# Thirty-two bytes over on the tiles of split weights and of the activations' pool

## The chip, the cores and the metric

The kernel runs on one core of a Trainium2 chip. The metric is the device time of one execution in microseconds (us), the median of several runs. Engines are named as in the profile: PE is TensorE, DVE is VectorE, ACT is ScalarE, POOL is GpSimd, and SP issues transfers.

## The reference

A decoder trunk of two layers on 256 tokens of width 1024, float32. Cut to what matters:

```
for each of 2 layers:
  h += 1/2 * (silu(n1 @ Wg1) * (n1 @ Wu1)) @ Wd1            # n1 = RMSNorm(h), hidden width 2816
  P  = RMSNorm(h) @ W_in                                    # one projection to all four mixers and the gates
  y  = retention(P), mamba2(P), latent_attention(P), differential_attention(P)   # each 256 x 512
  h += (sum_i sigmoid(gate_i) * (y_i @ W_branch_i)) @ W_out
  h += cross_attention(RMSNorm(h), RMSNorm(mem)) @ W_o      # 4 heads of 256
  h += 1/2 * (silu(n2 @ Wg2) * (n2 @ Wu2)) @ Wd2
return RMSNorm(h)
```

## The kernel before

Every large product is done in three passes of `float32r` matmuls. An operand is split into a part `hi` that fits `float32r` and a rest `lo`, and the product is hi·hi + lo·hi + hi·lo. For activations the function `split` (L346) makes the two parts, for weights `fetch` (L316) does: SP fetches a tile of 128 x 2048 numbers into `wr`, ACT copies it as `float32r` into `wh` (L334), and DVE subtracts to make `wl` (L335), in two halves. Each of the three pools `wr`, `wh` and `wl` has three buffers, so that one tile is used while the next is split and a third arrives.

`linear` (L351) holds activations as the stationary operand (`lhsT`, 128 x 128) and streams the weights (`rhs`, 512 columns); for each tile of weights and each of the two blocks of tokens it issues four matmuls of `wh` with `hi`, four of `wh` with `lo` and four of `wl` with `hi`:

```
for part, w in ((0, hi), (1, hi), (0, lo)):
    for k in range(m):
        pe.matmul(p_[b][:, :n], lhsT=xT(part, k0 + k)[:, b * P:(b + 1) * P], rhs=w[:, k * n:(k + 1) * n], ...)
```

`linear_t` (L371) is the other way round: the weights are stationary and 256 tokens are streamed, so the result comes transposed.

The activations come from two places. Normalized and transposed inputs of a stage are `xh0`, `xl0`, `xh1`, `xl1`, one buffer each of 128 x 1024 in the pool `xp`. Everything else of that size (`hid` of the feed-forward stages, the mixers' inputs and results such as `yrh` or `ymh`, the normalized memory `mmh`/`mml`, the cross attention's `xk`, `xq`, `xp`, `xo`) comes from `m4` (L171), a ring of eleven buffers in the pool `mp`. The pool `fp` has temporaries, among them a ring of five buffers of 128 x 512 handed out by `f2` (L180); `sp` has small tiles by name, handed out by `small` (L186).

The pools lie one behind the other in each partition's memory, in the order in which they are made: `cp` (constants and the residual `h`), `wr`, `wh`, `wl`, `xp`, `fp`, `sp`, `mp`. Inside a pool the tiles lie one behind the other, a tile's size rounded up to 32 bytes, and all the pools together fill nearly the whole of it. The order of the work is written out by hand: linears follow one another, and "chains" of smaller steps (transposes, softmax, the mixers' small matmuls) are advanced between them. The tables that both layers share (`tables`, L524) are one such chain near the start; the product `lp` of the differential attention's lambda belongs to it (L567 to L570).

Of the kernel before, what the change touches and what calls it, by code (L numbers as in the profile page):

```python
# [12 lines left out]
F32R = mybir.dt.float32r  # L13
# [3 lines left out]
PSUM = bass.MemoryType.PSUM  # L17
AX = mybir.AxisListType

P = 128  # L20
# [10 lines left out]
BUCKETS = 32  # L31
# tiles of weights that are made ready before the matmuls that are traced
AHEAD = 1

# columns of w_in by use
_sizes = (256, 256, 512, 512, 512, 1024, 8, 256, 128, 32, 512, 512, 512, 4096)
_at = np.concatenate([[0], np.cumsum(_sizes)])
(O_RQ, O_RK, O_RV, O_RG, O_Z, O_XBC, O_DT, O_CQ, O_CKV, O_KR, O_DQ, O_DK, O_DV, O_GL) = (int(v) for v in _at[:-1])
# groups of 512 columns, in the order in which they are streamed
G_QK, G_RV, G_RG, G_X0, G_X1, G_Z, G_DQ, G_DK, G_DV, G_GL = range(10)  # L40
_groups = [O_RQ, O_RV, O_RG, O_XBC, O_XBC + 512, O_Z, O_DQ, O_DK, O_DV] + [O_GL + 512 * i for i in range(8)]
MISC = 256 + 128 + 32 + 8

# per-partition parameters of one layer: (name, columns)
_pcols = [("ffn1", 8), ("mix", 8), ("xa", 8), ("mem", 8), ("ffn2", 8), ("ssm", 4), ("qn", 2), ("kvn", 1), ("dn", 1),
          ("cw", 32), ("cb", 8)]
# parameters that every partition needs, of one layer
_bcols = [("dtb", 8), ("alog", 8), ("dsk", 8), ("lam", 256)]
# [11 lines left out]
BO, NBC = _offsets(_bcols)  # L60
# constants that depend on shapes alone
CO, NCC = _offsets([("ident", 128), ("tri", 384), ("dmask", 256), ("inv", 48), ("sel", 8), ("dec", 4 * 256)])
# [37 lines left out]
def lay(x, mem, positions, **w):  # L100
    """The program's inputs: the arrays given, laid out; and constants."""
    a = {k: np.asarray(v) for k, v in w.items()}
# [45 lines left out]
def program(tc, a, out, upto="all"):  # L148
# [22 lines left out]
    def m4(name, dtype=F32):  # L171
        return mp.tile([P, 1024], dtype, tag="m", name=name)

# [14 lines left out]

    # ---- inputs that stay
    h = [[cp.tile([P, 512], F32, tag=f"h{b}{c}", name=f"h{b}{c}") for c in range(2)] for b in range(NB)]  # L190
# [31 lines left out]

    # ---- the order of work: linears one after another, and chains of smaller steps between them.
    # A chain yields how many half tiles of weights it lets pass, or what has to have happened before it goes on.
    chains = []
# [37 lines left out]

    # ---- weights, fetched in the order of use
    def chunks(srcs, kt, n):
# [43 lines left out]
    todo = list(plan())  # L309
    # a recent instruction of VectorE, for what is to be spread over the linears  # L310
    paced = None
    fetched = []
    # the last of the instructions that split weights, for what is to be queued behind it
    last = None

    def fetch(first=False):  # L316
        """The next tile of weights, as two float32r parts whose sum they are. The first one comes in pieces."""
        nonlocal last
        if not todo:
            return  # L320
        src, n = todo.pop(0)
        r = wr.tile([P, 2048], F32, tag="wr", name="wr")
        hi = wh.tile([P, 2048], F32R, tag="wh", name="wh")
        lo = wl.tile([P, 2048], F32R, tag="wl", name="wl")
        pieces = 4 if first else 2
        if not first:
            nc.sync.dma_start(r[:, :n], src)
        for i in range(pieces):
            s = slice(i * n // pieces, (i + 1) * n // pieces)
            if first:  # L330
                if i == 2:
                    nc.sync.dma_start(h[1][0], a["x"][1, :, :512])
                nc.sync.dma_start(r[:, s], src[:, s])
            last = act.activation(hi[:, s], r[:, s], AF.Copy)  # L334
            dve.tensor_tensor(lo[:, s], r[:, s], hi[:, s].bitcast(F32), ALU.subtract)  # L335
        fetched.append((hi, lo, n))
# [7 lines left out]

    # ---- building blocks
    def split(hi, lo, src):  # L346
        """hi + lo = src, in float32r; src is in SBUF or PSUM."""
        act.activation(hi, src, AF.Copy)
        dve.tensor_tensor(lo, src, hi.bitcast(F32), ALU.subtract)

    def linear(kt, n, xT, evacs):  # L351
        """Rows of tokens times weights [kt * 128, n], one or more; evac(b, psum) takes a block of rows."""
        ps = [[lin.tile([P, 512], F32, tag="lin", name="lin") for _ in range(NB)] for _ in evacs]
# [17 lines left out]
    def linear_t(xT, evac):  # L371
        """Weights [1024, 512] transposed times tokens: evac(i, psum) takes 256 columns as [128, 2, 256]."""
        ps = [lin.tile([P, 512], F32, tag="lin", name="lin") for _ in range(2)]
        for k0 in (0, 4):
            ws = weights(2048)
            for i in range(2):
                begin()
                for j in range(2):
                    for part, w in ((0, 0), (1, 0), (0, 1)):
                        for k in range(4):  # L380
                            o = k * 512 + (i * 2 + j) * P
                            # a start clears the flags of the whole bank: one for both halves
                            pe.matmul(ps[i][:, j * 256:(j + 1) * 256], lhsT=ws[w][:, o:o + P], rhs=xT(part, k0 + k),  # L383
# [6 lines left out]
    def transpose4(src, n=4):  # L390
        """Blocks of 128 columns of src, transposed, in one bank: [128, n, 128]."""
        ps = bank("tr")
# [4 lines left out]
    def split_gain(hi, lo, ps, gain, n=4):  # L397
        """hi + lo = a PSUM tile [128, n, 128] times a gain for each partition and n."""
        t = f2("sgt")[:, :n * P].rearrange("p (k t) -> p k t", k=n)
# [6 lines left out]
    def rstd_of(ss, n, m, name):  # L406
        """(ss / n + eps) ** -0.5 of m columns."""
        t = small("rs" + name, m)
# [9 lines left out]
    class Transposed:  # L418
        """src(b, c): [tokens, 512] for two blocks of columns, transposed and split; with a gain for each column.
        Each half starts as its columns are there."""  # L420

# [41 lines left out]
    def rows_of(r, name):  # L463
        """A value for each token, [P, NB], as rows [P, 256] alike on every partition."""
        ps = bank("rowp")
# [56 lines left out]

    # ---- tables that both layers share
    def tables():  # L524
# [19 lines left out]
        for b in range(NB):  # L544
# [18 lines left out]
            yield 2  # L563
        # lambda of the differential attention: -lambda for each layer
        for l in range(L):
            lp = bcol(l, "lam").rearrange("p (i e d) -> p i e d", i=2, e=2)
            pr = small("lp", 128).rearrange("p (i d) -> p i d", i=2)  # L567
            dve.tensor_tensor(pr, lp[:, :, 0], lp[:, :, 1], ALU.mult)
# [6 lines left out]
            dve.tensor_scalar(nlam[:, l:l + 1], nlam[:, l:l + 1], li, None, ALU.subtract)  # L575
        # relative bias, times 8, with the causal mask: [queries, head, (block 0, keys 0) (block 1, keys 0 and 1)]
        rel = relt[:, :384]
# [9 lines left out]
        for i, t in enumerate(_thresholds()):  # L587
            yield 3
            # not around the change of stage
            while 60 <= now < 72:  # L590
# [8 lines left out]
    def rope(dst, src, tb, n_heads, hf):  # L599
        """dst = src rotated, [P, heads, 2 * hf]; tb: [cos, sin, -sin] of hf columns each."""  # L600
        s = src.rearrange("p h (e d) -> p h e d", e=2)
# [12 lines left out]
    def attend(b, scores, masks, scale, sbt):  # L614
        """Softmax numerators of a block of queries, in sbt [P, n, 256]; the sums' reciprocals. scores: PSUM for each."""
        n, nk = len(scores), (b + 1) * P
# [10 lines left out]
    def probs_t(pT, b, probs):  # L627
        """Transposed probabilities of a block of queries; pT: keys 0 [P, 4, 256] and keys 1 [P, 4, 128]."""
        for kb in range(b + 1):
# [5 lines left out]
    def mixers(l, xT, nxt):  # L635
# [10 lines left out]

        # -- retention
        qk = [f2("qk") for _ in range(NB)]
# [61 lines left out]

        # -- MLA's low ranks, and Mamba's steps
        dtx = small("dtx", 16).rearrange("p (b h) -> p b h", b=2)
# [23 lines left out]
        def mamba():  # L736
            yield ["misc"]
            x = dtx.rearrange("p b h -> p (b h)")
            e, z1, z2, p_ = (small(n, 16) for n in ("sp0", "sp1", "sp2", "sp3"))
            # softplus(x) = max(x, 0) + 2 artanh(e / (2 + e)) with e = exp(-|x|)  # L740
            dve.scalar_tensor_tensor(e, x, -1.0, x, ALU.mult, ALU.min)
# [24 lines left out]
            dve.tensor_copy(gc, pg[:, :16])  # L766
            # the running sums in two parts, for each block of tokens
            gr = sp.tile([P, NB, 16], F32R, tag="gr", name="gr", bufs=1)
# [3 lines left out]
            yield ["x0", "x1"]  # L772
            # xs on tokens
            xdt, xD = two("xdt"), two("xD")
# [65 lines left out]

        # -- Mamba-2: convolution, on channels
        for j in range(2):
# [19 lines left out]

        # -- gates and merge
        mg = []
# [30 lines left out]

        # -- MLA
        qT, kT, v = heads("mqT"), heads("mkT"), two("mv")
# [68 lines left out]

        # -- differential attention
        def on_rows(dst, name):
# [75 lines left out]

    # ---- memory, normalized, transposed and split
    def memory(l, mem, before):
# [187 lines left out]
```

## Time and profile before

| | |
|---|---|
| time, median of 3 runs | 1603.86 us (1603.84 to 1603.92) |
| span of the profiled execution | 1601.6 us, 20813 instructions |
| between that span and the median of the runs | 2.3 us |
| busy: PE, DVE, ACT, POOL | 99%, 67%, 52%, 2% of the span |
[...]
| share of the 16 DMA engines, weights' queue | 50.2% |

The span runs from the first to the last instruction of one profiled execution. Busy time of PE counts overlapping matmuls, so a PE that is busy all the time may still run at different paces.

### The profile page before, as it was taken

The page shows a single profiled execution, that of the slowest core. Times are in us where ns is not written, and L with a number is a line of the kernel's source. Part 1 is how long each engine was busy: PE and PEld are TensorE (multiplying, and loading weights), DVE is VectorE, ACT ScalarE, POOL GpSimd, SP SyncE. Part 2 cuts the span into 40 slices and gives each one's busy share as a digit, 9 for nine tenths or more (in the row PEclk, how much of TensorE's full clock was granted, in tenths as well). Part 3 has the DMA queues.
Part 4 walks back from the last instruction along what each step waited for, and adds up shares of the span by engine and source line. Part 5 has one row for each costly group of instructions (what it writes and reads, how often), then busy time and mean ns, then how long its engine had stood idle before and what let it go on. Part 6 is the DMA issues. An engine that isn't in the chain of part 4 may idle for free.

```text
span 1601.6 us, 20813 instructions
## 1 busy us (share of the span) xinstructions
PE 1587.3 (99%) x8236; PEld 1349.4 (84%) x8236; DVE 1070.4 (67%) x1698; ACT 825.2 (52%) x1221; POOL 27.0 (2%) x39
## 2 busy tenths in 40 slices
PE   8999999999999999999999999999999999999998
PEld 6888889898888988888888888898988899888886
DVE  6787699998777666554465546697656766565543
ACT  6544446656655545444454444475575554454432
POOL 0000000000000000000000000000000000000000
PEclk9999999999999999999999999999999999999999
DMA  7555554454555544555555556444545554455541
GB/s 288 200 178 187 185 175 159 151 169 147 204 184 169 181 155 162 184 184 175 186 192 185 183 174 207 149 158 152 184 150 206 184 183 163 155 177 180 195 171 66
DMA packets 41713, 281.58 MB, mean 176 GB/s; under 512 B 4624, under 2 KB 5008, under 8 KB 9488
## 3 DMA queue, kind: packets, MB, share of 16 engines
q1 hardware_dynamic: 39600, 275.07, 50.2%
q10 hardware_dynamic: 2016, 5.19, 1.0%
q8 instruction: 64, 1.05, 0.3%
q14 instruction: 33, 0.27, 0.0%
HBM read 279.20 MB, written 1.05 MB: 175 GB/s over the span
## 4 chain that ended last, share of the span: by engine, by line
PE 98%; ACT 0%; DMA 0%; issue 0%; DVE 0%; SPq 0%; POOLq 0%; POOL 0%
PE lin L365 78%; PE lin L383 11%; PE tr L394 2%; PE ht L500 1%; PE xs L1094 1%; PE xo L1140 1%; PE up L905 1%; PE my L821 0%; PE ds L990 0%; DMA h<-x 0%; PE ms L941 0%; PE pt L632 0%; ACT wh L334 0%; PE my L823 0%; PE do L1013 0%
## 5 line engine op out<-in xcount | busy, mean ns | idle before, releaser
L335 DVE TENSOR_TENSOR wl<-wr,wh 128x1024 fp32r<-128x1024 f32 (+2 forms) x534 | 624.9, 1195 | 388.1 <-ACT wh L334 385.6
L334 ACT ACTIVATE wh<-wr 128x1024 fp32r<-128x1024 f32 (+2 forms) x534 | 533.4, 1033 | 518.5 <-PE lin L365 398.7
L365 PE MATMUL lin<-wh,xh 128*128 128x512 f32 (+1 forms) x1216 | 334.0, 396 | 0.2 <-ACT wh L334 0.2
L365 PE MATMUL lin<-wh,xl 128*128 128x512 f32 (+1 forms) x1216 | 325.9, 390 | 0.0
L365 PE MATMUL lin<-wl,xh 128*128 128x512 f32 (+1 forms) x1216 | 325.1, 389 | 0.0
L365 PEld LDWEIGHTS lin<-wh,xl 128*128 128x128 f32 x1216 | 228.8, 188 | 48.1
L365 PEld LDWEIGHTS lin<-wl,xh 128*128 128x128 f32 x1216 | 228.8, 188 | 47.7
L365 PEld LDWEIGHTS lin<-wh,xh 128*128 128x128 f32 x1216 | 222.5, 189 | 43.6 <-ACT wh L334 1.2
L365 PE MATMUL lin<-wh,hid 128*128 128x512 f32 x704 | 180.4, 396 | 0.0
L365 PEld LDWEIGHTS lin<-wh,hid 128*128 128x128 f32 x704 | 131.6, 188 | 31.4
L365 PE MATMUL lin<-wl,hid 128*128 128x512 f32 x352 | 97.7, 395 | 0.0
L365 PEld LDWEIGHTS lin<-wl,hid 128*128 128x128 f32 x352 | 66.1, 188 | 16.0
L510 ACT ACTIVATE sg<-lin,rffn 128x256 f32<-128x256 f32 x88 | 40.9, 464 | 65.2 <-PE lin L365 65.1
L596 DVE SCALAR_TENSOR_TENSOR bias<-relt,d,bias 128x384 f32<-128x384 f32 x124 | 69.8, 612 | 0.8
L383 PE MATMUL lin<-xh,wh 128*128 128x256 f32 x384 | 63.2, 287 | 0.0
L383 PE MATMUL lin<-xh,wl 128*128 128x256 f32 x384 | 61.7, 283 | 0.0
L383 PE MATMUL lin<-xl,wh 128*128 128x256 f32 x384 | 61.7, 283 | 0.0
L511 DVE SCALAR_TENSOR_TENSOR toks<-lin,rffn,sg 128x256 f32<-128x256 f32 x88 | 42.3, 481 | 25.7 <-ACT sg L510 25.7
L383 PEld LDWEIGHTS lin<-xh,wh 128*128 128x128 f32 x384 | 53.1, 191 | 0.3
L383 PEld LDWEIGHTS lin<-xh,wl 128*128 128x128 f32 x384 | 53.0, 192 | 0.0
L383 PEld LDWEIGHTS lin<-xl,wh 128*128 128x128 f32 x384 | 52.9, 191 | 0.0
L416 ACT ACTIVATE junk<-h 128x512 bf16<-128x512 f32 x36 | 22.4, 621 | 31.2 <-DVE h L484 17.2
(385 smaller groups left out, 1536.7 us busy)
## 6 DMA issues: line engine op xcount, KB each, us to landing
wr<-gu SPq DMA_DIRECT2D x87, 1024.0 KB, 5.0
wr<-win SPq DMA_DIRECT2D x68, 1024.0 KB, 5.0
wr<-dn SPq DMA_DIRECT2D x40, 1024.0 KB, 4.8
wr<-wbr SPq DMA_DIRECT2D x16, 1024.0 KB, 4.9
wr<-w_out SPq DMA_DIRECT2D x8, 1024.0 KB, 4.9
wr<-xa_wk SPq DMA_DIRECT2D x8, 1024.0 KB, 5.0
wr<-xa_wq SPq DMA_DIRECT2D x8, 1024.0 KB, 4.9
wr<-xa_wv SPq DMA_DIRECT2D x8, 1024.0 KB, 4.9
```

Of the source, the lines that this page charges most:

```text
L334: last = act.activation(hi[:, s], r[:, s], AF.Copy)
L335: dve.tensor_tensor(lo[:, s], r[:, s], hi[:, s].bitcast(F32), ALU.subtract)
L365: pe.matmul(p_[b][:, :n], lhsT=xT(part, k0 + k)[:, b * P:(b + 1) * P], rhs=w[:, k * n:(k + 1) * n], start=first, stop=last)
L383: pe.matmul(ps[i][:, j * 256:(j + 1) * 256], lhsT=ws[w][:, o:o + P], rhs=xT(part, k0 + k), start=k0 + k + part + w + j == 0, stop=k0 + k = ...
L394: pe.transpose(ps[:, k * P:(k + 1) * P], src[:, k * P:(k + 1) * P], ident)
L416: act.activation(j[:, :src.free_size()], src, AF.Square, accum_out=out_)
L500: pe.transpose(ps[:, k, blk(b)], toks[:, b, k * P:(k + 1) * P], ident)
L510: act.activation(sg, ps[:, :256], AF.Silu, scale=xT.r[:, b:b + 1])
L511: paced = dve.scalar_tensor_tensor(toks[:, b], ps[:, 256:], xT.r[:, b:b + 1], sg, ALU.mult, ALU.mult)
L596: dve.scalar_tensor_tensor(bias[:, hd], ge, d8[:, hd, i + 1:i + 2], bias[:, hd], ALU.mult, ALU.add)
L905: pe.matmul(ps[:, :n], lhsT=lowT[p_][:, k0 + k, blk(b)], rhs=wm[w][:, o + k * n:o + (k + 1) * n], start=i == 0, stop=i == len(seq) - 1)
L1094: pe.matmul(ps[:, j], lhsT=q[part][:, 2 * j + k, blk(b)], rhs=kT[c][w][:, 2 * j + k], start=not part + w + k, stop=w + k == 2)
```

## The change

Three kinds of tiles are allocated with 8 more columns of 4 bytes, and used without them: those of `wh`, of `wl`, and the eleven buffers of `m4`. The small tile `lp` (128 columns) is no longer one of `sp`'s but takes a buffer of the ring of `f2`. The rest of the diff drops comments.

```
     def m4(name, dtype=F32):
-        return mp.tile([P, 1024], dtype, tag="m", name=name)
+        return mp.tile([P, 1024 + 8], dtype, tag="m", name=name)[:, :1024]
...
         r = wr.tile([P, 2048], F32, tag="wr", name="wr")
-        hi = wh.tile([P, 2048], F32R, tag="wh", name="wh")
-        lo = wl.tile([P, 2048], F32R, tag="wl", name="wl")
+        hi = wh.tile([P, 2048 + 8], F32R, tag="wh", name="wh")[:, :2048]
+        lo = wl.tile([P, 2048 + 8], F32R, tag="wl", name="wl")[:, :2048]
...
             lp = bcol(l, "lam").rearrange("p (i e d) -> p i e d", i=2, e=2)
-            pr = small("lp", 128).rearrange("p (i d) -> p i d", i=2)
+            pr = f2("lp")[:, :128].rearrange("p (i d) -> p i d", i=2)
```

## Rows read from the trace of the kernel before

**Rows 1.** The page's first lines: span, busy time, share of the span and instructions of each engine; and the granted TensorE clock in 40 slices of the span, in tenths.

```profile
span 1601.6 us, 20813 instructions
PE 1587.3 (99%) x8236; PEld 1349.4 (84%) x8236; DVE 1070.4 (67%) x1698; ACT 825.2 (52%) x1221; POOL 27.0 (2%) x39
...
PEclk9999999999999999999999999999999999999999
```

**Rows 2.** The page's chain that ended last, shares of the span by engine and by line.

```profile
PE 98%; ACT 0%; DMA 0%; issue 0%; DVE 0%; SPq 0%; POOLq 0%; POOL 0%
PE lin L365 78%; PE lin L383 11%; PE tr L394 2%; PE ht L500 1%; PE xs L1094 1%; PE xo L1140 1%; PE up L905 1%; PE my L821 0%; PE ds L990 0%; DMA h<-x 0%; PE ms L941 0%; PE pt L632 0%; ACT wh L334 0%; PE my L823 0%; PE do L1013 0%
```

**Rows 3.** Groups of matmuls by line and shape: engine, operation, out<-in by the program's names, shape, count | busy us, mean ns of one | idle before. Of the 18 groups of 32 on `y` and `xo` tiles the first and the last stand here.

```profile
L365 PE MATMUL lin<-wh,xh 128*128 128x512 f32 x1184 | 326.6, 397 | 0.2 <-ACT wh L334 0.2
L365 PE MATMUL lin<-wh,xl 128*128 128x512 f32 x1184 | 318.4, 391 | 0.0
L365 PE MATMUL lin<-wl,xh 128*128 128x512 f32 x1184 | 317.6, 390 | 0.0
...
L365 PE MATMUL lin<-wh,hid 128*128 128x512 f32 x704 | 180.4, 396 | 0.0
...
L365 PE MATMUL lin<-wl,hid 128*128 128x512 f32 x352 | 97.7, 395 | 0.0
...
L383 PE MATMUL lin<-xh,wh 128*128 128x256 f32 x384 | 63.2, 287 | 0.0
L383 PE MATMUL lin<-xh,wl 128*128 128x256 f32 x384 | 61.7, 283 | 0.0
L383 PE MATMUL lin<-xl,wh 128*128 128x256 f32 x384 | 61.7, 283 | 0.0
...
L383 PE MATMUL lin<-mmh,wh 128*128 128x256 f32 x128 | 20.0, 278 | 0.0
...
L365 PE MATMUL lin<-wh,mmh 128*128 128x512 f32 x64 | 17.9, 400 | 0.0
...
L365 PE MATMUL lin<-wh,ymh 128*128 128x512 f32 x32 | 9.1, 406 | 0.0
...
L365 PE MATMUL lin<-wl,xo1h 128*128 128x512 f32 x32 | 8.7, 394 | 0.0
```

**Rows 4.** Timeline of PE in a gate and up projection, 62.6 to 74.5 us: start in us, us from the first start to the last end of the group, engine, line, out<-in, count. The pace is the distance between two starts.

```profile
62.64 0.60 PE L500 MATMUL ht<-ident,toks 128*128 128x128 f32 x4
63.00 1.17 PE L365 MATMUL lin<-wh,xh 128*128 128x512 f32 x4
64.01 1.09 PE L365 MATMUL lin<-wh,xl 128*128 128x512 f32 x4
64.93 1.07 PE L365 MATMUL lin<-wl,xh 128*128 128x512 f32 x4
65.84 1.07 PE L365 MATMUL lin<-wh,xh 128*128 128x512 f32 x4
...
73.10 1.07 PE L365 MATMUL lin<-wl,xh 128*128 128x512 f32 x4
74.01 0.60 PE L500 MATMUL ht<-ident,toks 128*128 128x128 f32 x4
```

**Rows 5.** The same view of the last down projection, 1538 to 1602 us, first and last of the rows used; 204 matmuls lie between the starts at 1540.88 and 1588.47.

```profile
1540.88 2.03 PE L365 MATMUL lin<-wh,hid 128*128 128x512 f32 x8
...
1588.47 2.03 PE L365 MATMUL lin<-wh,hid 128*128 128x512 f32 x8
```

**Rows 6.** The same view of `linear_t`: on `xh`/`xl` (251 us) and on `mmh`/`mml` (514 us).

```profile
250.93 0.64 PE L383 MATMUL lin<-xh,wl 128*128 128x256 f32 x4
251.41 0.64 PE L383 MATMUL lin<-xh,wh 128*128 128x256 f32 x4
...
514.15 0.62 PE L383 MATMUL lin<-mmh,wl 128*128 128x256 f32 x4
...
516.42 0.28 PE L383 MATMUL lin<-mml,wh 128*128 128x256 f32 x1
```

**Rows 7.** The same view of the cross attention's scores, 550 to 553 us, first row and the row behind the last (24 matmuls between).

```profile
550.00 0.64 PE L1094 MATMUL xs<-xk0h,xq 128*128 128x256 f32 x4
...
552.83 0.41 PE L383 MATMUL lin<-xh,wh 128*128 128x256 f32 x2
```

**Rows 8.** The two groups that split weights, by line and shape, columns as in rows 3, with what ended the idle time before them.

```profile
L335 DVE TENSOR_TENSOR wl<-wr,wh 128x1024 fp32r<-128x1024 f32 x502 | 600.2, 1220 | 368.0 <-ACT wh L334 367.3
L334 ACT ACTIVATE wh<-wr 128x1024 fp32r<-128x1024 f32 x502 | 511.5, 1053 | 484.5 <-PE lin L365 371.0 <-issue 85.3 <-PE lin L383 22.6
```

**Rows 9.** The instructions on the tile `lp`: line, engine, operation, count: duration in ns min/median/max, first and last start in us.

```profile
L568 DVE TENSOR_TENSOR lp<-bcs x2: 285/285/285, 35.5 to 37.0; 128x128 f32<-128x128 f32 x2
L570 DVE TENSOR_REDUCE ls<-lp x2: 280/280/280, 36.3 to 38.5; 128x2 f32<-128x128 f32 x2
```

**Rows 10.** The timeline of PE at 424 columns (240 to 249 us, first row and the row behind the last, 48 matmuls between) and at 384 columns (328.67 us; six up to the next row shown).

```profile
239.82 0.94 PE L365 MATMUL lin<-wh,xh 128*128 128x424 f32 x4
...
249.10 1.04 PE L394 MATMUL tr<-ident,yr 128*128 128x128 f32 x8
...
328.67 0.52 PE L905 MATMUL up<-wh,lowh 128*128 128x384 f32 x2
...
329.73 0.28 PE L905 MATMUL up<-wh,lowh 128*128 128x256 f32 x1
```

## The prediction

> **What bounds the kernel now.** I read the page's first lines, then its chain, then the groups of instructions, then stretches of the timeline of TensorE (PE). The page says that PE is busy for 99% of the span at the full granted clock [rows 1]. The chain that ended last is PE for 98%, of which 78% are the matmuls of line 365 (`linear`) and 11% those of line 383 (`linear_t`) [rows 2]: the time is the number of matmuls times the pace at which one follows another. Busy time doesn't show that pace: the mean of one matmul is 390 to 397 ns because neighbours overlap [rows 3]. The pace is the distance between the starts of two groups in the timeline, divided by the matmuls between them.
>
> Read so, matmuls of one width have more than one pace:
> - 512 columns, stationary operand from the tiles `xh`/`xl`, moving operand from `wh`/`wl`: the first twelve after a break by transposes take 2.84 us (63.00 to 65.84), then 32 take 7.26 us, 226.9 ns each. Over 64.01 to 74.01, with most of the recovery in it, 10.00 us / 44 = 227.3 ns [rows 4].
> - 512 columns, stationary operand from the pool `mp` (`hid`): from 1540.88 to 1588.47, 47.59 us for 204 matmuls, 233.3 ns, right from the first group on [rows 5].
> - 256 columns (`linear_t`): with `xh` as moving operand 0.48 us for four, 120.0 ns; with `mmh`/`mml` (pool `mp`) 2.27 us for 20, 113.5 ns [rows 6]. At L1094, where the operands come from `mp` and `mg`, 2.83 us for 24, 117.9 ns [rows 7].
>
> Clock, shape and data type are alike within each width. What differs is where the operands lie, and that is what the change moves.
>
> **Where the tiles lie.** I add up the tiles in the order of the pools. `wr`, `wh`, `wl`, `xp` and `fp` hold only multiples of 512 bytes, so all their tiles begin at one place of a 512-byte line; call it 0. The small tiles of `sp` add up to 320 bytes more than a multiple of 512, so each tile of `mp` begins at 320. "Moving less stationary" is then 0 for `linear` on `xh`/`xl`, 192 for `linear` on `hid` and its like, 0 for `linear_t` on `xh`/`xl`, and 320 for `linear_t` on `mmh`/`mml`.
>
> After the change the three buffers of `wh` begin at 0, 32 and 64, those of `wl` at 96, 128 and 160, all of `xp` and `fp` at 192 (six times 32). `sp` loses 512 bytes with `lp`, so the eleven buffers of `mp` begin at 0, 32, ... 320. No pair of a weight tile and an `xh`/`xl` tile begins at one place any more (moving less stationary: 320 to 480). With an `mp` tile the difference takes many values, and is 0 for 6 of the 66 pairs.
>
> **The change part by part.**
> 1. *No instruction is added or removed.* Shapes, queues and waits stay; `n` elements of each padded tile are used as before.
> 2. *ScalarE and VectorE write `wh` and `wl` at other places.* Line 334 takes 1053 ns and line 335 takes 1220 ns for 1024 columns; VectorE is busy for 67% of the span, and before these instructions the two engines sat idle for 368 and 485 us, mostly waiting for PE [rows 8]. I cost a change here at nothing: the work that hides it is PE's. Were line 335 a tenth slower, its 600 us would grow by 60 us inside 368 us of slack. No row shows such a loss.
> 3. *`lp` moves from `sp` to the ring of five `f` buffers.* Its four instructions take 285 and 280 ns each on VectorE at 35.5 to 38.5 us [rows 9], and by the code only the norm's four `sgt` tiles have used the ring by then. They queue on VectorE as before: nothing either way.
> 4. *`linear` on `xh`/`xl`*, 3 × 1184 = 3552 matmuls of 512 columns [rows 3], now 227.3 ns. The trace has no such matmul with unequal starts. From below: the pace stays, nothing. From above: the pace of the only 512-column matmuls with unequal starts, 233.3 ns, +6.0 ns × 3552 = +21.3 us. Between them lie the matmuls of 424 and 384 columns. At 424 columns each next `k` moves the moving operand by 1696 bytes, 160 past a multiple of 512, so they see several differences in turn: 9.28 us for 48, 193.3 ns, and they don't settle. At 384 columns (difference 192) six take 1.06 us, 176.7 ns [rows 10]. That is 16.6 ns for 40 columns; carried on by 88 columns it gives 193.3 + 36.6 = 230 ns for 512. After the change the difference holds for four or eight matmuls, then steps by 96 bytes between `wh` and `wl`: partly like the `hid` rows, partly like the 424 rows. I take the middle, 231.65 ns: +4.35 × 3552 = +15.5 us.
> 5. *`linear` on tiles of `mp`*: 704 + 352 on `hid`, 3 × 64 on `mmh`/`mml`, 18 groups of 32 on `y` and `xo` tiles, 1824 together [rows 3], now 233.3 ns. From above: they stay, 0. From below: those find the pace of `xh`, −6.0 × 1824 = −10.9 us. With a different pair of places for nearly every tile they come nearest to the 424 columns, 230 ns: −3.3 × 1824 = −6.0 us.
> 6. *`linear_t`*: 1152 matmuls on `xh`/`xl` [rows 3] leave equal starts. From 120.0 to 113.5 would be −7.5 us, staying is 0; the nearest row is L1094's 117.9 ns, unequal starts that don't settle lower: −2.1 × 1152 = −2.4 us. 384 on `mmh`/`mml` [rows 3] lose their settled 113.5 for the same 117.9: +4.4 × 384 = +1.7 us; bounds 0 and, at 120.0, +2.5 us.
>
> Sum: 15.5 − 6.0 − 2.4 + 1.7 = **+8.8 us**. The span shown is 1601.6 us, and 2.3 us lie around it up to the median of 1603.86; no part of the change touches these. 1603.9 + 8.8 = 1612.7 us. The bounds together: −10.9 − 7.5 = −18.4 (1585.5) and 21.3 + 2.5 = +23.8 (1627.7).
>
> The rows show 120.0 and 113.5 ns for the same 256-column shape with operands in different tiles. [...]
>
> **The rivals.**
> *A: equal starts are the harm (faster).* [...] For it: at 256 columns equal starts are the slowest, 120.0 against 117.9 and 113.5 [rows 6, 7]. Against it: at 512 columns equal starts are the fastest, 226.9 against 233.3 [rows 4, 5], and these are three quarters of the time. It gives −7.5 for `linear_t` and up to −10.9 for part 5, with part 4 at 0: 1585 to 1597 us. It decides from the point where `linear` on `xh` keeps 227.3 ns or less.
> *B: places don't matter (no change).* The paces could come from how PE restarts after a break, not from addresses. [...] Against it: `hid` runs at 233.3 ns for over 200 matmuls with no break in the weights' rhythm [rows 5]. It gives 1603.9 us.
> *C: every unequal pair costs as `hid` does.* Then part 4 is +21.3 and part 5 nothing: 1622 to 1627 us. For it: the one difference that the trace shows at 512 columns. Against it: 424 columns, with four differences in turn, carry on to only 230 ns [rows 10].
>
> **How the numbers follow.** My forecast (pace of `linear` on `xh` between 229 and 232 ns, `mp` between 229 and 233) 0.37; C 0.15; A 0.28; B 0.20. A measurement of this kernel can tell about 0.2%, 3.2 us, from no change. Slower is the forecast and C, 0.52; same is B, 0.20; faster is A, 0.28. The predicted time is the forecast's, 1612.7, with a range of its own of 1607 to 1620. The range of 1590 to 1626 holds the forecast, B, nearly all of C and over half of A.
>
> **What would show it.** In the changed profile: `linear` on `xh` starts four matmuls every 0.92 to 0.93 us where it now takes 0.91, with no settled 226.9; `hid` starts twelve every 2.76 us where it now takes 2.80; `linear_t` on `xh` four every 0.47 us; lines 334 and 335 keep their durations; the chain stays PE for 98%; the instruction counts are the same. I am wrong if `linear` on `xh` keeps or betters 0.91 us for four (A or B), or if VectorE's line 335 grows and PE begins to wait for it.

## The result, and the profile after

The changed kernel takes 1617.73 us (median of four runs, 1617.07 to 1618.63) where the kernel before took 1603.85 us beside it: 13.9 us more, a ratio of 1.009 (95% interval 1.0076 to 1.0105). It is slower by more than the 0.2% that a measurement of this kernel can tell. The profiled execution's span is 1616.7 us, 15.1 us longer than that of before [rows 1]; it is the slowest of the four runs, so the spans differ by a little more than the medians.

The first lines of the page of the changed kernel, and the first line of its chain:

```profile
span 1616.7 us, 20813 instructions
...
PE 1602.1 (99%) x8236; PEld 1350.8 (84%) x8236; DVE 1069.8 (66%) x1698; ACT 826.4 (51%) x1221; POOL 27.1 (2%) x39
...
PEclk9999999999999999999999999999999999999999
...
PE 97%; DMA 1%; DVE 1%; ACT 0%; issue 0%; SPq 0%; POOLq 0%; POOL 0%; ACTq 0%; DVEq 0%
```

Every count of instructions is that of before, the mean granted clock is 0.999 in both profiles, and PE, busy for 99% here too, has no pauses to speak of: its matmuls follow one another more slowly. The diff moves the lines by one, so `linear` is now line 366, `linear_t` 384, and the two that split weights 335 and 336.

The timeline of PE in a gate and up projection, the stretch that answers to [rows 4] (columns as there):

```profile
64.32 0.60 PE L501 MATMUL ht<-ident,toks 128*128 128x128 f32 x4
64.68 1.18 PE L366 MATMUL lin<-wh,xh 128*128 128x512 f32 x4
65.69 1.07 PE L366 MATMUL lin<-wh,xl 128*128 128x512 f32 x4
...
67.53 1.07 PE L366 MATMUL lin<-wh,xh 128*128 128x512 f32 x4
...
70.29 1.09 PE L366 MATMUL lin<-wh,xh 128*128 128x512 f32 x4
...
74.02 1.08 PE L366 MATMUL lin<-wh,xl 128*128 128x512 f32 x4
```

The first twelve behind the transposes take 2.85 us, as before (2.84). Then nothing settles at 226.9 ns any more: 2.76 us for the twelve from 67.53 (230.0 ns) and 3.73 us for the sixteen from 70.29 (233.1 ns).

The last down projection, which answers to [rows 5]; 204 matmuls lie between these starts too:

```profile
1556.27 2.01 PE L366 MATMUL lin<-wh,hid 128*128 128x512 f32 x8
...
1603.59 2.02 PE L366 MATMUL lin<-wh,hid 128*128 128x512 f32 x8
```

47.32 us for 204 matmuls, 232.0 ns, where it was 233.3.

`linear_t` on `xh`/`xl` (52 matmuls between the two rows) and on `mmh`/`mml` (12 between), which answer to [rows 6]:

```profile
254.72 0.65 PE L384 MATMUL lin<-xh,wh 128*128 128x256 f32 x4
...
260.90 0.64 PE L384 MATMUL lin<-xl,wh 128*128 128x256 f32 x4
...
514.83 0.63 PE L384 MATMUL lin<-mmh,wh 128*128 128x256 f32 x4
...
516.24 0.63 PE L384 MATMUL lin<-mmh,wh 128*128 128x256 f32 x4
```

118.8 and 117.5 ns, where it was 120.0 and 113.5.

The groups that split weights, which answer to [rows 8]: the same durations and the same slack.

```profile
L336 DVE TENSOR_TENSOR wl<-wr,wh 128x1024 fp32r<-128x1024 f32 x502 | 600.0, 1220 | 376.3 <-ACT wh L335 376.1
L335 ACT ACTIVATE wh<-wr 128x1024 fp32r<-128x1024 f32 x502 | 512.4, 1055 | 491.8 <-PE lin L366 378.7 <-issue 84.6 <-PE lin L384 22.9
```

Single stretches are not enough to share out 15 us, so from here on the pace of a kind is the mean distance of starts over all its matmuls in a trace (the few longer gaps at breaks left out). It is worked out from the trace's starts, and each gain or loss is this mean's difference times the number of matmuls:

| kind | matmuls | before, ns | after, ns | us |
|---|---|---|---|---|
| `linear` on `xh`/`xl` | 3552 | 227.7 | 232.5 | +17.1 |
| `linear` on tiles of `mp` | 1824 | 233.3 | 232.1 | −2.3 |
| `linear_t` on `xh`/`xl` | 1152 | 119.9 | 118.5 | −1.6 |
| `linear_t` on `mmh`/`mml` | 384 | 113.9 | 118.1 | +1.6 |
| sum | | | | +14.8 |

The sum is within 0.3 us of the difference of the spans. The loss is matmul pace, to about 1 us, and it lies in `linear` on `xh`/`xl`: the other three kinds together give back 2.3 us.

### The profile page after: what moved, and what is told of

It is laid out like the page before. It is cut to its first block, busy times and chain, and to the rows that moved or that the text cites. A ratio compares the mean times of both kernels' runs of the same rounds, so it can differ in the third digit from the quotient of the medians.

```text
span 1616.7 us, 20813 instructions
## 1 busy us (share of the span) xinstructions
PE 1602.1 (99%) x8236; PEld 1350.8 (84%) x8236; DVE 1069.8 (66%) x1698; ACT 826.4 (51%) x1221; POOL 27.1 (2%) x39
## 4 chain that ended last, share of the span: by engine, by line
PE 97%; DMA 1%; DVE 1%; ACT 0%; issue 0%; SPq 0%; POOLq 0%; POOL 0%; ACTq 0%; DVEq 0%
PE lin L366 77%; PE lin L384 11%; PE tr L395 2%; PE ht L501 1%; PE xs L1095 1%; PE xo L1141 1%; PE up L906 1%; DMA cst<-consts 1%; PE my L822 0%; PE ds L991 0%; DMA h<-x 0%; PE ms L942 0%; DMA wr<-gu 0%; ACT wh L335 0%; DVE wl L336 0%
## 5 line engine op out<-in xcount | busy, mean ns | idle before, releaser
L366 PE MATMUL lin<-wh,xh 128*128 128x512 f32 (+1 forms) x1216 | 339.0, 400 | 0.2 <-ACT wh L335 0.2
L366 PE MATMUL lin<-wh,xl 128*128 128x512 f32 (+1 forms) x1216 | 331.5, 394 | 0.0
L366 PE MATMUL lin<-wl,xh 128*128 128x512 f32 (+1 forms) x1216 | 331.4, 394 | 0.0
```

## The experiments

Each kernel is the kernel before with tiles moved in memory. None leaves any work out. "Distance" is the place of the moving operand less that of the stationary one, as in the prediction, for `linear`; for `linear_t` the same tiles have the opposite sign. In the kernel before it is 0 for `xh`/`xl` and 192 for tiles of `mp`. Times without an interval are single runs; the kernel before took 1602.45 us beside the first four kernels, 1604.93 beside the next four, 1602.57 beside `x32_m480`, `x160_m96` and `m_only`, and 1603.04 beside `w_256`.

### Does the place matter at all, and which side: one_place and swap

`one_place` adds one unused tile of 192 bytes to the pool of the small tiles (it is made first, so it lies ahead of them, which makes no difference to `mp`), so that `mp` begins at 0 like all the rest, and one `memset` of that tile. Every distance is 0. Rival B says that nothing happens.

```
     pool.memset(mhalf, -0.5)
+    pool.memset(sp.tile([P, 48], F32, tag="gap", name="gaps", bufs=1), 0.0)
```

> The kernel before with one unused tile of 192 bytes behind sp's small tiles, so that the pool mp also begins at place 0 of a 512-byte line: all weight tiles, xh/xl and mp tiles at one place, and no padding. Theory P (the pace belongs to the places of the stationary and the moving operand relative to each other): linear on mp tiles falls from 233.3 to about 227.3 ns (1824 x 6.0 = -10.9 us), linear_t on mmh/mml rises from 113.9 to 120 ns (384 x 6.1 = +2.3 us), linear on xh stays: about -8.6 us, 1595 us. Rival K (the pace belongs to the stage, its rhythm and its pool, not to the places): nothing moves, 1604 us.

1593.78 us (1593.43 to 1594.61), a ratio of 0.9944 (0.9928 to 0.9961): faster. The timeline of PE in its last down projection:

```profile
1576.98 1.98 PE L366 MATMUL lin<-wh,hid 128*128 128x512 f32 x8
1578.79 1.07 PE L366 MATMUL lin<-wl,hid 128*128 128x512 f32 x4
1579.70 1.98 PE L366 MATMUL lin<-wh,hid 128*128 128x512 f32 x8
```

Twelve take 2.72 us, 226.7 ns, on the same tiles that took 233.3 [rows 5]. Nothing but the small tiles and `mp` has moved: B is out. Over all tiles of `mp` it is 227.1 ns, −11.3 us for 1824; `linear_t` on `mmh`/`mml` pays +2.3 us for it (119.9 ns).

`swap` gives the distance to `xh`/`xl` (320) and takes it from `mp` (0).

```
     pool.memset(mhalf, -0.5)
+    pool.memset(xp.tile([P, 48], F32, tag="gap", name="gapx"), 0.0)
...
-            pr = small("lp", 128).rearrange("p (i d) -> p i d", i=2)
+            pr = f2("lp")[:, :128].rearrange("p (i d) -> p i d", i=2)
```

> No tile is padded; an unused tile of 192 bytes ahead of xh/xl and lp moved to the f ring, so that xh/xl begin at 192 and mp at 0, weights at 0: the two kinds of stationary tiles change roles, each with one constant difference (moving less stationary 320 for xh/xl, 0 for mp). Theory P: linear on mp falls to about 227 ns (-11 us), linear on xh leaves 227.7; if 320 costs as 192 does it goes to 233.3 (3552 x 5.6 = +20 us), linear_t on xh falls below 120 (-2 to -7 us): about 1605 to 1615 us. Theory S (what costs is a start that changes from tile to tile, any constant difference settles): linear on xh settles at 227 or below, 1595 us or less. Rival K: 1604 us, both paces as before.

1594.83 us, no worse than `one_place`. The timeline of PE in a gate and up projection, and in `linear_t` on `xh`/`xl`:

```profile
64.07 1.07 PE L366 MATMUL lin<-wh,xl 128*128 128x512 f32 x4
...
74.14 0.60 PE L501 MATMUL ht<-ident,toks 128*128 128x128 f32 x4
...
254.75 0.64 PE L384 MATMUL lin<-xh,wh 128*128 128x256 f32 x4
...
257.10 0.64 PE L384 MATMUL lin<-xh,wl 128*128 128x256 f32 x4
...
261.90 0.62 PE L384 MATMUL lin<-xh,wl 128*128 128x256 f32 x4
...
265.98 0.62 PE L384 MATMUL lin<-xh,wl 128*128 128x256 f32 x4
```

`linear` takes 10.07 us for 44, 228.9 ns: a distance of 320 costs 1.5 ns on the mean (229.2), not the 6 that 192 cost. So "unequal" is not one thing, and neither of the two theories above (233.3 ns, or 227 and below) had this pace. And `linear_t` takes 2.35 us for 20, 117.5 ns, ahead of a break by transposes and 4.08 us for 36, 113.3 ns, behind it: at 256 columns the same tiles at the same distance have two paces, and 115.5 is the mean over all of them. Against `one_place`, `swap` pays +5.8 us in `linear` on `xh`/`xl` (1.62 ns × 3552) and gets −5.1 us back in `linear_t` (4.39 × 1152): a tie.

### Which part of the change: w_only, m_only and w_64

`w_only` leaves `m4` as it was, `m_only` leaves `wh` and `wl` as they were; both move `lp`.

```
-        hi = wh.tile([P, 2048], F32R, tag="wh", name="wh")
-        lo = wl.tile([P, 2048], F32R, tag="wl", name="wl")
+        hi = wh.tile([P, 2048 + 8], F32R, tag="wh", name="wh")[:, :2048]
+        lo = wl.tile([P, 2048 + 8], F32R, tag="wl", name="wl")[:, :2048]
```

> Only the weight tiles get the 32 bytes (with lp moved), the pool mp unpadded at place 0; xh/xl at 192 as in the changed kernel. Theory P and theory S alike: linear on xh goes to the changed kernel's 232.5 ns (+17 us); linear on mp, with differences 0 to 160 that change from wh to wl, about 232 ns (-2 us): about 1617 us, all of the loss. If the padded mp made the loss: 1604 us.

```
-        return mp.tile([P, 1024], dtype, tag="m", name=name)
+        return mp.tile([P, 1024 + 8], dtype, tag="m", name=name)[:, :1024]
```

> The one half of the change alone: only the tiles of m4 get the 32 bytes (with lp moved), the weights unpadded, xh/xl at 0 as before. Linear on xh stays at 227.7 ns and linear_t on xh at 119.9; linear on mp goes over the eleven places, mean of the curve 229 to 233 ns (-2 to -7 us); linear_t on mmh/mml 117 to 119 (+1 to +2 us): about 1599 to 1603 us. If the change of place from tile to tile costs by itself, linear on mp above 232: 1603 us or more.

`w_only` takes 1617.68 us, the time of the whole change; `m_only` 1602.32 us, the time of the kernel before beside it. The loss is the weights' padding alone. It isn't the shift of `xh`/`xl` that goes with it: `swap` has `xh`/`xl` at 192 and `mp` at 0 just as `w_only` has, with all weights at 0, and takes 1594.83 us. From `swap` to `w_only` only weight tiles move, and `linear` goes from 229.2 to 232.5 ns on `xh`/`xl` and from 227.2 to 232.0 on `mp`. So the place of the stationary tile alone doesn't set the pace; that of the moving one counts as well. In `m_only` the eleven places of `mp` tiles bring `linear` on them from 233.3 to 232.0 ns (−2.4 us) and lose 1.6 us in `linear_t` on `mmh`/`mml`.

`w_64` is `w_only` with 64 bytes, so that the six weight buffers stand 64 bytes apart.

```
-        hi = wh.tile([P, 2048], F32R, tag="wh", name="wh")
-        lo = wl.tile([P, 2048], F32R, tag="wl", name="wl")
+        hi = wh.tile([P, 2048 + 16], F32R, tag="wh", name="wh")[:, :2048]
+        lo = wl.tile([P, 2048 + 16], F32R, tag="wl", name="wl")[:, :2048]
```

> The weight tiles get 64 bytes over in place of 32 (lp moved, mp unpadded): wh at 0, 64, 128, wl at 192, 256, 320, xh/xl at 384, mp at 192. Theory P with an average over differences: as w_only, linear on xh about 232 ns, about 1617 us. Theory S with a step of 64 bytes that doesn't disturb (all starts stay alike modulo 64 bytes): linear on xh settles between the old paces, 227 to 230 ns, about 1604 to 1608 us.

1612.74 us, between the two theories: 231.9 ns on `xh`/`xl`, 231.5 on `mp`. The size of the step matters: with 32 bytes it was 232.5 and 232.0. To say how, one distance at a time has to be held through a whole kernel.

### One distance at a time: six kernels

Each has an unused tile ahead of the tiles of `xp` (`gapx`), some also one ahead of those of `sp` (`gaps`), and all move `lp`. A column is 4 bytes. The name gives the places at which `xp`'s activations and `mp` begin; the weights stay at 0, so the distance for `linear` is 512 less that place.

```
     pool.memset(mhalf, -0.5)
+    pool.memset(xp.tile([P, 64], F32, tag="gap", name="gapx"), 0.0)             # x256_m64
+    pool.memset(xp.tile([P, 112], F32, tag="gap", name="gapx"), 0.0)            # x448_m384, and 32 columns in sp
+    pool.memset(xp.tile([P, 16], F32, tag="gap", name="gapx"), 0.0)             # x64_m256, and 96 columns in sp
+    pool.memset(xp.tile([P, 32], F32, tag="gap", name="gapx"), 0.0)             # x128_m448
+    pool.memset(xp.tile([P, 8], F32, tag="gap", name="gapx"), 0.0)              # x32_m480, and 32 columns in sp
+    pool.memset(xp.tile([P, 40], F32, tag="gap", name="gapx"), 0.0)             # x160_m96, and 32 columns in sp
```

> No padded tiles; unused tiles ahead of xh/xl and lp moved, so that xh/xl begin at 256 and mp at 64, weights at 0 (moving less stationary: 256 for linear on xh/xl, 448 for linear on mp). Theory P1 (equal places are the best for 512 columns, any other constant difference costs 229 to 233.3 ns, and for 256 columns equal places are the worst): linear on xh 229 to 233 ns (+6 to +20 us), linear on mp 229 to 233 (-8 to 0), linear_t on xh 113 to 118 (-2 to -7): 1600 to 1615 us. Theory P2 (the pace is a curve over the difference that may fall below 226.9 away from 0): one of the two below 226 ns.

> As the run with xh/xl at 256, with xh/xl at 448 and mp at 384 (moving less stationary: 64 for linear on xh/xl, 128 for linear on mp). Theory P1: linear on xh 229 to 233 ns, linear on mp 229 to 233, linear_t on xh 113 to 118: 1600 to 1615 us. Theory P2: one of the two below 226 ns.

> As before, with xh/xl at 64 and mp at 256 (moving less stationary: 448 for linear on xh/xl, 256 for linear on mp). If the places alone set the pace, linear on xh here has the pace that linear on mp has in the run with mp at 64, and linear on mp that of linear on xh in the run with xh/xl at 256, each within 0.7 ns (breaks between stages differ); if the stage sets it, they differ by more. 1600 to 1615 us.

> As before, with xh/xl at 128 and mp at 448 (moving less stationary: 384 for linear on xh/xl, 64 for linear on mp). If the places alone set the pace, linear on mp has the pace of linear on xh in the run with xh/xl at 448 within 0.7 ns. Theory P1: linear on xh 229 to 233 ns, 1600 to 1615 us; theory P2: below 226 ns.

> No padded tiles; xh/xl at 32 and mp at 480, weights at 0 (moving less stationary: 480 for linear on xh/xl, 32 for linear on mp). From the runs so far the pace repeats every 256 bytes: 0 and 256 give 227.6 ns, 64 and 320 give 229.2, 128 and 384 give 232.7, 192 and 448 give 233.4. If it is one curve over the difference modulo 256: 480 (as 224) lies between 233.4 and 227.6, 32 between 227.6 and 229.2, linear on xh about 230.5, linear on mp about 228.4: about 1604 us. If steps of 32 bytes have a cost of their own (half of a 64-byte step): both above 231.5, about 1613 us.

> No padded tiles; xh/xl at 160 and mp at 96, weights at 0 (moving less stationary: 352, that is 96 modulo 256, for linear on xh/xl, 416, that is 160, for linear on mp). One curve over the difference modulo 256: 96 about 231 ns, 160 about 233 ns: about 1612 us. If steps of 32 bytes have a cost of their own: both above 233.4, about 1622 us.

The timeline of PE of `x256_m64` in a gate and up projection; 36 matmuls lie between the two rows:

```profile
64.74 1.07 PE L366 MATMUL lin<-wh,xh 128*128 128x512 f32 x4
...
72.91 0.60 PE L501 MATMUL ht<-ident,toks 128*128 128x128 f32 x4
```

8.17 us for 36, 226.9 ns: at a distance of 256 the pace is that of distance 0 [rows 4]. The tiles of the two operands begin at different places here, just as the change arranges it, and nothing is lost (1602.63 us against 1604.93 beside it).

The last down projection of `x64_m256` (distance 256 for `mp`) and then of `x160_m96` (distance 416 for `mp`):

```profile
1594.87 1.98 PE L367 MATMUL lin<-wh,hid 128*128 128x512 f32 x8
...
1597.59 1.98 PE L367 MATMUL lin<-wh,hid 128*128 128x512 f32 x8
```

```profile
1607.20 2.04 PE L367 MATMUL lin<-wh,hid 128*128 128x512 f32 x8
...
1610.01 2.04 PE L367 MATMUL lin<-wh,hid 128*128 128x512 f32 x8
```

Twelve in 2.72 us (226.7 ns) and in 2.81 us (234.2 ns): the same instructions on the same tiles. And `x32_m480` on `xh`/`xl` (distance 480), 40 matmuls between the rows:

```profile
65.73 1.10 PE L367 MATMUL lin<-wh,xl 128*128 128x512 f32 x4
...
75.06 1.10 PE L367 MATMUL lin<-wl,xh 128*128 128x512 f32 x4
```

9.33 us for 40, 233.3 ns from the first group behind the break on.

All kernels side by side, in the mean paces (ns) of the four kinds, in the order of the table above. "Sum" is what the paces make against those of before, with the counts of that table; "span" is the difference of the profiled spans.

| kernel | distance `x` | distance `mp` | paces | sum, us | span, us | time, us |
|---|---|---|---|---|---|---|
| before | 0 | 192 | 227.7, 233.3, 119.9, 113.9 | | | 1603.85 |
| after | 320 to 480 | many | 232.5, 232.1, 118.5, 118.1 | +14.8 | +15.1 | 1617.73 |
| `one_place` | 0 | 0 | 227.5, 227.1, 119.9, 120.0 | −9.5 | −8.9 | 1593.78 |
| `swap` | 320 | 0 | 229.2, 227.2, 115.5, 120.0 | −8.7 | −8.9 | 1594.83 |
| `w_only` | 320 to 480 | many | 232.5, 232.0, 118.5, 118.4 | +14.7 | +14.0 | 1617.68 |
| `m_only` | 0 | many | 227.7, 232.0, 119.9, 118.0 | −0.9 | −1.3 | 1602.32 |
| `w_64` | 128 to 448 | many | 231.9, 231.5, 117.7, 117.8 | +10.5 | +9.2 | 1612.74 |
| `x256_m64` | 256 | 448 | 227.7, 233.3, 119.9, 113.9 | 0.0 | −1.1 | 1602.63 |
| `x448_m384` | 64 | 128 | 229.2, 232.6, 114.9, 118.6 | +0.2 | −0.3 | 1603.35 |
| `x64_m256` | 448 | 256 | 233.4, 227.4, 117.3, 119.9 | +8.4 | +9.0 | 1612.61 |
| `x128_m448` | 384 | 64 | 232.9, 229.3, 118.9, 117.8 | +11.5 | +11.3 | 1614.97 |
| `x32_m480` | 480 | 32 | 233.2, 233.3, 116.8, 118.3 | +17.7 | +17.8 | 1621.45 |
| `x160_m96` | 352 | 416 | 233.4, 234.1, 117.8, 119.9 | +21.6 | +21.6 | 1625.21 |
| `w_256` | 0, 256 | 0, 256 | 227.5, 227.1, 119.9, 120.0 | −9.5 | −9.7 | 1593.53 |

Two things follow. The sums meet the spans within 1.3 us everywhere, so to about that much the paces of these matmuls are all that differs. And in these kernels the pace at 512 columns is the same within 0.6 ns at two distances 256 bytes apart, whichever pool the stationary operand is in: 227.1 to 227.7 at distances 0 and 256; 229.2 to 229.3 at 64 and 320; 232.6 to 232.9 at 128 and 384; 233.3 to 233.4 at 192 and 448; 233.2 to 233.4 at 32, 352 (96) and 480 (224); 234.1 at 416 (160). The odd multiples of 32 have no second distance 256 bytes away in these constant-distance kernels, so for them this is not shown. A rival by which a pace belongs to the stage or the pool is out: the tiles of `mp` show at 64 and 256 what `xh`/`xl` show there (229.3 and 229.2 ns, 227.4 and 227.7), and the other way round. At 256 columns (`linear_t`) equal places are at the slow end, 119.9 to 120.0, and the others lie between 113.9 and 119.9, all of them means; in `swap` the mean of 115.5 was made of two paces. There the distance alone doesn't fix the mean: at 64 it is 113.9 ns on `mmh`/`mml` (`x256_m64`, and before at 320) and 117.3 on `xh`/`xl` (`x64_m256`).

Several expectations missed. At 256 neither P1 (229 to 233 ns) nor P2 (under 226) holds, and no kernel has a mean pace under 226 at 512 columns. `x32_m480` takes 1621.45 us, beyond both of its cases (1604 and 1613), and `x160_m96` 1625.21, beyond both of its own (1612 and 1622): the paces at 32, 96 and 160 lie above those of both neighbours. The exchange of roles held: `x64_m256` and `x128_m448` repeat the paces of the other pool within 0.3 ns.

### Different places without a loss: w_256

If distances 256 bytes apart cost alike, buffers may begin at different places as long as these differ by 256. `w_256` pads `wh` by 256 bytes, moves `lp`, and has the first activation, whose result nothing reads, write into an existing tile, which frees the 64 bytes of the small tile `begin` (two buffers of 32), so that `mp` meets the same places. All distances are 0 or 256.

```
-        hi = wh.tile([P, 2048], F32R, tag="wh", name="wh")
+        hi = wh.tile([P, 2048 + 64], F32R, tag="wh", name="wh")[:, :2048]
...
-    act.activation(small("begin", 1), mhalf[:, :1], AF.Silu)
+    act.activation(nlam[:, :1], mhalf[:, :1], AF.Silu)
```

> The wh tiles get 256 bytes over in place of 32, so that neighbouring buffers begin at different places of a 512-byte line (0, 256, 0) but at one place of 256 bytes; wl and xh/xl begin at 256, mp at 0; lp moved, and the first Silu's result goes to another small tile to make room. If the pace goes by the difference of places modulo 256 bytes: all differences are 0, linear on xh stays at 227.6 ns although its tiles begin at different places from buffer to buffer, linear on mp falls to 227.2, linear_t 119.9 throughout: as with all at one place, 1594 us, 0.994 of before. If different places of a 512-byte line, or the change from buffer to buffer, cost by themselves: linear on xh at 229 ns or more, 1600 us or more.

1593.53 us (1593.36 to 1594.72), a ratio of 0.9942 (0.9928 to 0.9955). The timeline of PE in a gate and up projection, 32 matmuls between the rows:

```profile
65.36 1.07 PE L365 MATMUL lin<-wh,xh 128*128 128x512 f32 x4
...
72.61 1.07 PE L365 MATMUL lin<-wl,xh 128*128 128x512 f32 x4
```

7.25 us for 32, 226.6 ns. So distances 0 and 256 cost alike also where they change from buffer to buffer (227.5 ns on `xh`/`xl`, as in `one_place`), and this kernel and `one_place` are both some 0.6% faster than the kernel before, with no difference between them that can be told.

## Why the prediction was right, and where its terms were off

The direction and the place of the loss hold: equal starts of weights and `xh`/`xl` are lost, and `linear` on them goes from 227.7 to 232.5 ns. The prediction took too much as costly, though: it counted places modulo 512 bytes and every unequal pair as a loss, and `x256_m64` and `w_256` have pairs 256 bytes apart at 227.7 and 227.5 ns, no cost. The time lies in the forecast's own range of 1607 to 1620, 5.0 us above its value. By its steps:

1. *No instruction added*: holds, every count is the same.
2. *Splitting costs nothing*: holds, 1055 and 1220 ns, and idle time of 492 and 376 us before them.
3. *`lp`*: holds. The instructions on it, in the changed kernel (columns as in [rows 9]):

```profile
L569 DVE TENSOR_TENSOR lp<-bcs x2: 283/284/284, 38.9 to 40.4; 128x128 f32<-128x128 f32 x2
L571 DVE TENSOR_REDUCE ls<-lp x2: 275/276/278, 39.7 to 41.9; 128x2 f32<-128x128 f32 x2
```

   They start 3.4 us later than before, durations are the same, and the runs that move `lp` without padding the weights (`m_only`, `x256_m64`) lose nothing.
4. *`linear` on `xh`/`xl`*: taken at 231.65 ns, measured 232.5: +17.1 us where +15.5 stood. The prediction thought of `hid`'s pace with some of it given back by changes of place. The six kernels say it otherwise: `wh` stands at distances 320, 352 and 384, `wl` at 416, 448 and 480. By the paces that these distances have when they are held throughout, that is 2/3 × (229.2 + 233.4 + 232.8) / 3 + 1/3 × (234.1 + 233.4 + 233.2) / 3 = 232.4 ns. What made it less than `hid`'s 233.3 is, by this reckoning, the one cheap distance, 320. The reckoning fits the mean better than its parts: sorted by weight buffer (three in turn, in the order of fetching), the changed kernel's own starts give 230.4 ns at 320, 234.3 at 352, 232.5 at 384, 233.6 at 416, 232.2 at 448 and 232.2 at 480.
5. *`linear` on tiles of `mp`*: this is the mis-sized term. It stood at −6.0 us and measured −2.3: 232.1 ns instead of 230. The step that failed is the one that carried the 424-column pace on by 88 columns. The 424-column matmuls themselves run at 193.5 ns after the change and 193.3 before, and say nothing about 512 columns. The mean of the paces over the eight multiples of 32 within 256 bytes is (227.4 + 233.3 + 229.2 + 233.4 + 232.8 + 234.1 + 233.4 + 233.2) / 8 = 232.1 ns, and that is what eleven places against six measured. Some of this agreement is luck: for `mp` in `w_only`, with distances 0 to 160, the same reckoning as in point 4 gives 231.1 ns where 232.0 was measured.
6. *`linear_t`*: −1.6 and +1.6 us, against −2.4 and +1.7. The neighbour's row, L1094's 117.9 ns, was a fair guess for both (118.5 and 118.1).

The terms were short by 1.6 (4), 3.7 (5) and 0.7 us (6), together 6.0; so the sum came to 8.8 where the paces make 14.8.

Of the rivals, C came nearest: it had the tiles of `mp` staying at 233.3, which is 1.3 ns off, and `xh`/`xl` joining them, which is 0.8 ns off. That puts it at 1622 and above, 4 us over the measurement. "Every unequal pair costs as `hid` does" is nearly true for most measured distances (232.6 to 234.1 ns), but not for 256 (227.4 to 227.7) and for 64 (229.2 to 229.3, 320 with it). A needed `linear` on `xh`/`xl` to keep 227.3 ns and fell at that point; its argument holds for 256 columns alone, where `swap` gains 5.1 us by unequal places and pays more for it at 512. B is out by `one_place`: 192 unused bytes move the time by 0.6%.

Of the signs that the prediction named, `linear` on `xh`/`xl` starts four every 0.91 to 0.94 us with no settled 226.9, `hid` starts twelve every 2.78 (2.76 was named), `linear_t` four every 0.47. The chain is PE for 97%, not 98%, with 1% each for DMA and DVE.

B let the paces come from how PE restarts after a break. That was the author's guess: the runs show slower matmuls behind transposes (2.84 us for the first twelve before, 2.85 after), and none shows that breaks make the difference between stages. With shape and count alike and a granted clock of 0.998 to 0.999, the 512-column matmuls have mean paces of 227.1 to 234.1 ns in these runs, by where the two operands lie.

Open is why distances 256 bytes apart cost alike, and why the others cost more. The traces show when matmuls start, and no run shows the cause of their distance.

In `w_64`, where the distance changes between `wh` and `wl` and from buffer to buffer, the pace is a little above what its distances make: it runs at 231.9 ns on `xh`/`xl` where the paces of its distances, weighted as in point 4, make 2/3 × (232.8 + 233.4 + 227.6) / 3 + 1/3 × (229.2 + 232.8 + 233.4) / 3 = 231.4. Its timeline of PE shows eight matmuls on a `wh` tile at distance 256 that follow four on `wl` at 448:

```profile
71.31 1.09 PE L365 MATMUL lin<-wh,xh 128*128 128x512 f32 x4
72.24 1.07 PE L365 MATMUL lin<-wh,xl 128*128 128x512 f32 x4
73.14 1.10 PE L365 MATMUL lin<-wl,xh 128*128 128x512 f32 x4
```

The first four take 0.93 us, the next four 0.90. Over all eights at 256 on `xh`/`xl` in this run the first four have 231.7 ns on the mean and the last four 228.1, where 256 held throughout gives 227.7. So in this run the cheap distance, held for a few matmuls only, is not as cheap as in the table; why is open.

## What to carry to other kernels

Work out where the stationary and the moving operand of the costly matmuls begin, and compare the distance of starts in the timeline between stages with the same shape: in the kernel before, `linear` on tiles of `mp` was 2.5% slower than on `xh`/`xl` (233.3 against 227.7 ns) at a granted clock of 0.999, and other addresses alone brought it to 227.1 (`one_place`). In these kernels the 512-column matmuls were fastest at distances 0 and 256 (227.1 to 227.7 ns), and padding by 32 bytes cost 0.9% where an unused tile of 192 bytes gained 0.6%. Before a pace is carried over from another width, look for a stage of the same width: carried from 424 columns to 512 it came to 230 ns where 232.1 was measured.

## What the runs showed of the hardware

- In these kernels the mean pace of the 512-column `float32r` matmuls of `linear`, each with a weight load of its own, goes with the distance between the operands' places: 227.1 to 227.7 ns at 0 and 256, 229.2 to 229.3 at 64 and 320, 232.6 to 232.9 at 128 and 384, 233.3 to 233.4 at 192 and 448. The odd multiples of 32 were measured at one distance each: 233.3 ns at 32, 233.4 at 352, 234.1 at 416 and 233.2 at 480. The prediction counted places modulo 512 bytes; distances 256 bytes apart measured alike.
- At 256 columns (`linear_t`) it is the other way round: equal places give 119.9 to 120.0 ns, the slow end, and most other distances less (113.9 to 118.9), but one distance had different means in different stages (113.9 in `x256_m64` and 117.3 in `x64_m256`, both at 64).
- At 256 columns the same tiles at one distance held two paces in `swap`, 117.5 ns ahead of a break by transposes and 113.3 behind it; the mean over all is 115.5.
- In `w_64` the first four 512-column matmuls behind a change to distance 256 have 231.7 ns on the mean and the next four 228.1, where 256 held throughout gives 227.7 (`x256_m64`).
